# Recurrent gates by blocks of 64 features: two stacked float32r passes in place of one float32 product, issued in steps

## The chip, the core and the metric

The kernel runs on one core of one Trainium2 chip. The metric is the device time of one execution in microseconds (us), from the first to the last instruction with the launch around it. Before the change it is 2330.84 us, the median of three runs (2327.64, 2333.63 and 2330.84).

## The reference

The reference is a backbone of two layers. Each layer normalises and modulates 1280 tokens (256 of context, 1024 latent), multiplies them by one wide input weight, feeds four parallel branches (attention, a diagonal state space model called S5, a gated recurrence called RG-LRU, and pooling), gates and projects each branch, sums them and adds the result to the stream. The change touches the RG-LRU, whose gates are two block-diagonal products with four blocks of 64 features:

```python
def _rglru_states(x, h0, lam, w_a, b_a, w_x, b_x, reverse):
    r = jax.nn.sigmoid(_block_diag(x, w_a, b_a))
    i = jax.nn.sigmoid(_block_diag(x, w_x, b_x))
    log_a = -LRU_C * r * jax.nn.softplus(-lam)
    a = jnp.exp(log_a)
    b = jnp.sqrt(-jnp.expm1(2.0 * log_a)) * (i * x)
    return _real_scan(a, b, h0, reverse)
```

It runs in both directions over the sequence, and the sum of both is the branch. Outputs are float32.

## The kernel before, in words

Features lie on the 128 partitions and tokens along the free axis, in three chunks of 256, 512 and 512 tokens (`CH`; the first is the context). A big product keeps float32 accuracy by splitting each operand into a high part in the format float32r and a low part, the rest; `gemm` (L165) then makes three passes for each 128 rows of the contraction: low weights by high input, high by low, high by high. `hgemm` does this for one tile of 128 output features by one chunk with eight such groups, so 24 passes, into a PSUM bank of pool `pg` (two banks). Weights come by `load_w` (L158): a DMA into a ring of two raw tiles (`wr`), a copy by ScalarE to the high part and a subtraction by VectorE to the low part (`wh` and `wl`, four tiles each).

The order within a layer is written in `layer` (L1124): `mla_in`, `mla_kv`, `s5_in` and `lru_in` (input products and what follows on them), then `lru`, `cq_in` (the query latent), `mla_q` (queries), `pool_in`, `pool` with two `gate` tiles between its halves, then `attention`, the other six gates, the S5 branch, the logits of the first merge branch, `merge` and `out_proj`. A program orders the instructions of each engine ahead of time by priority, which is the order in the text except where `hp` raises it, and lets an engine take later work that its own costs call ready. On the chip each engine then keeps that order and waits where an input is late. The gates, and after them the logits, depend on nothing but the modulated input and a weight tile.

`lru` (L584) first computes constants of the recurrence on small tiles and loads `wg`, all gate weights of the layer, as 128 by 128 matrices that hold two blocks of 64 on the diagonal and zeros elsewhere. For each half of the features (f) and each direction (d), four pairs a layer, it does the following. For each chunk and each of the two gates, one float32 matmul of 128 by 128 weights with `xl` writes a bank (pool `pm`, two banks, for the first gate; pool `pS`, three banks, for the second), and ScalarE's tanh writes it to `l1` (tr) or `l2` (ti). Over all 1280 tokens then come exp, tanh and square on ScalarE, a multiply on VectorE, a square root on ScalarE (with a table load before and after), two multiplies and a scan on VectorE. `l1` to `l4` have one buffer each, so the next pair's tanh waits for the scan before. `pool` uses `l1` to `l3` after that. Scratch memory is a stack of pools: `pr` and `pa` for the part up to the pooling, in whose place `p5` (S5), `pt` (attention), `pc` (merge) and `pd` (output projection) come later, a tile there waiting for the tiles that lay in its bytes before. `stream` and `whl` are never released.

Of the kernel before, what the change touches and what calls it, by code (L numbers as in the profile page):

```python
# [16 lines left out]
F32 = mybir.dt.float32  # L17
F32R = mybir.dt.float32r
# [21 lines left out]


V_BADA, V_G, V_QN, V_KVN, V_QG, V_KG, V_KRG = 0, 24, 32, 34, 35, 37, 38
V_D, V_CW, V_CB, V_LAM, V_BA, V_BX, V_PB, V_PS = 39, 41, 49, 51, 55, 59, 63, 65
NV = 67

def view(ap, *dims):

# [16 lines left out]
class Net:  # L64
# [90 lines left out]
        self.act(hi, src, AF.Identity, scale=gain)  # L155
        self.stt(lo, src, gain, hi.bitcast(F32), ALU.mult, ALU.subtract)

    def load_w(self, src, nk, small=False):  # L158

        m = src.shape[1] // nk  # L160
        out = []
        with self.hp():
            for i in range(0, nk * m, 512):
                n = min(512, nk * m - i)
                raw = self.wraw.tile([128, 512], F32, tag="wr", name=self.name("wr"))  # L165
                th, tl, w, kw = ("wph", "wpl", 256, {"bufs": 2}) if small else ("wh", "wl", 512, {})
                hi = self.whl.tile([128, w], F32R, tag=th, name=self.name(th), **kw)
                lo = self.whl.tile([128, w], F32R, tag=tl, name=self.name(tl), **kw)
                self.dma(raw[:, 0:n], src[:, i:i + n])
                self.split(hi[:, 0:n], lo[:, 0:n], raw[:, 0:n])  # L170
                out += [(hi[:, c:c + m], lo[:, c:c + m]) for c in range(0, n, m)]
        return out
# [254 lines left out]
                self.act(vv[:, 256 * i:256 * i + 256], ps[:, 256 * i:256 * i + 256], AF.Identity, scale=rkv[:, t + i:t + i + 1])  # L427
            self.dma(m["vD"][:, t:t + 2], view(vv, 2, 4, 64))

    def cq_in(self, l, m, lat, pa):  # L430

        vec, sv = self.vec[l], m["sums"]
        m["cq"] = [view(self.t(pa, n_, 2 * NT, dt=F32R), 2, NT) for n_ in ("lat", "lat2")]
        sq0 = self.t(pa, "xp", 1312, 2)
        for f in range(2):
            w = self.load_w(self.I["w_in"][l, 1 + f], NK)
            for ci in lat:
                s0, n = CH[ci]
                ps = self.hgemm(w, ci)
                sq = sq0[:, s0:s0 + n] if f == 0 else self.sc(n)  # L440
                with self.hp():
                    self.gain_split(m["cq"][0][:, f, s0:s0 + n], m["cq"][1][:, f, s0:s0 + n], ps, vec[:, V_QN + f:V_QN + f + 1])
                    self.act(sq, ps, AF.Square)
                if f == 1:
                    with self.hp():
                        self.tt(sq, sq, sq0[:, s0:s0 + n], ALU.add)
                    self.tok_sums(sv[:, 2, s0 // 128:(s0 + n) // 128], [sq], self.ones)

    def mla_q(self, l, m, lat, pa):

# [131 lines left out]
        return out  # L582

    def lru(self, l, xls, oD, outs, pa, pr):  # L584
        nc, I, vec = self.nc, self.I, self.vec[l]
        sp = self.t(pa, "lsp", 36)
        lam = vec[:, V_LAM:V_LAM + 4]
        e, z, z2, acc, p4, m4 = (sp[:, 4 * i:4 * i + 4] for i in range(6))
        hba = sp[:, 24:32]
        self.stt(e, lam, -1.0, lam, ALU.mult, ALU.max)  # L590
        self.act(e, e, AF.Exp, scale=-1.0)
        self.ts(z, e, 2.0, None, ALU.add, None)
        nc.vector.reciprocal(out=z, in_=z)
        self.tt(z, z, e, ALU.mult)
        self.tt(z2, z, z, ALU.mult)
        nc.vector.memset(acc, 1.0 / 17)
        for d in (15, 13, 11, 9, 7, 5, 3, 1):
            self.tt(acc, acc, z2, ALU.mult)
            self.ts(acc, acc, 1.0 / d, None, ALU.add, None)
        self.tt(acc, acc, z, ALU.mult)  # L600
        self.ts(z2, lam, -1.0, 0.0, ALU.mult, ALU.max)
# [3 lines left out]
        self.ts(hba, vec[:, V_BA:V_BA + 8], 0.5, None, ALU.mult, None)  # L605
        wg = self.t(pa, "wg", 1024)
        self.dma(wg, I["w_lru"][l])
        wgv = view(wg, 2, 2, 2, 128)
        for f in range(2):
            xl = xls[f]  # L610
            y = self.t(pr, "ly", NT)
            for d in range(2):
                c = 2 * d + f
                col = lambda a: a[:, c:c + 1]
                tr, ti, a, th = (self.t(pr, n_, w_)[:, 0:NT] for n_, w_ in (("l1", 1312), ("l2", 1312), ("l3", 8 * SC), ("l4", 8 * SC)))
                for s0, n in CH:
                    for g, dst in ((0, tr), (1, ti)):
                        ps = (self.pS() if g else self.ps())[:, 0:n]
                        self.mm(ps, wgv[:, d, g, f], xl[:, s0:s0 + n])
                        self.act(dst[:, s0:s0 + n], ps, AF.Tanh, bias=hba[:, 4 * g + c:4 * g + c + 1], scale=0.5)  # L620
                self.act(a, tr, AF.Exp, bias=col(m4), scale=col(m4))
                self.act(th, tr, AF.Tanh, bias=col(p4), scale=col(p4))
                self.act(tr, a, AF.Square)
                self.stt(th, tr, 1.0, th, ALU.add, ALU.mult)
                self.act(th, th, AF.Sqrt, scale=0.25)
                self.stt(ti, ti, 1.0, xl, ALU.add, ALU.mult)
                self.tt(ti, ti, th, ALU.mult)
                scan = nc.vector.tensor_tensor_scan
                if d == 0:
# [7 lines left out]
            o0 = CH[outs[0]][0]  # L637
            self.dma(oD[f][:, o0:], y[:, o0:])


    def pool_in(self, l, lat, pa):

        out = []
        for f in range(2):
            w = self.load_w(self.I["w_in"][l, 5 + f], NK)
            xp = self.t(pa, "xp", 1312, 2)
            for c, n in ((0, 8), (264, 16), (1304, 8)):
                self.nc.gpsimd.memset(xp[:, c:c + n], 0.0)
            for ci in lat:
                s0, n = CH[ci]  # L650
                ps = self.hgemm(w, ci)
                off = s0 + 8 + (16 if ci else 0)
                with self.hp():
                    self.act(xp[:, off:off + n], ps, AF.Copy)
            out.append(xp)
        return out

# [362 lines left out]
    def merge(self, l, lat, oD, gD, tD, pc, s5):  # L1020
# [5 lines left out]
        for bi, b in enumerate(ORDER):  # L1026
# [3 lines left out]
            for ci in lat:  # L1030
                s0, n = CH[ci]
                for f in range(2):
                    with self.hp(2000):
                        o, gt = (self.stream.tile([128, 512], F32, tag="og", name=self.name("og"), bufs=2)[:, 0:n] for _ in range(2))
                        self.dma(o, oD[b][f][:, s0:s0 + n])
                        self.dma(gt, gD[b][f][:, s0:s0 + n])
                        self.stt(o, o, BSCALE[b], gt, ALU.mult, ALU.mult)
# [1 line left out]
            for j in range(NK):  # L1039
                if bi > 0:  # L1040
                    w = self.load_w(I["w_in"][l, 17 + 8 * b + j], NK)
                else:
                    a0 = CH[lat[0]][0]
                    self.dma(y[j][:, a0:], tD[j][:, a0:])
                wp = self.load_w(I["w_branch"][l, b, j], 2, True)
                for ci in lat if j < NK - 1 else [1] + [c for c in lat if c != 1]:
                    s0, n = CH[ci]
                    if bi > 0:
# [40 lines left out]
    def out_proj(self, l, groups, xsrc, pd, xs, acc, bg):  # L1089
        last = l == DEPTH - 1  # L1090
        for grp in groups:
# [4 lines left out]
            for j in range(NK):  # L1096
                w = self.load_w(self.I["w_out"][l, j], NK)
                for ci in grp:
                    s0, n = CH[ci]
                    c = 1 if ci == 0 else 0  # L1100
                    with self.hp(2000):
                        x0 = self.stream.tile([128, 512], F32, tag="og", name=self.name("ox"), bufs=2)[:, 0:n]
                        self.dma(x0, xsrc[:, j, s0:s0 + n])
                    ps = self.hgemm(w, ci)
                    x = x0 if last else xs[ci][:, j]
# [18 lines left out]
    def layer(self, l, pre):  # L1124
# [4 lines left out]
        with self.phase("pr") as pr, self.phase("pa") as pa:  # L1129
# [2 lines left out]
            self.mla_kv(l, m, pa)  # L1132
            uF, uD = self.s5_in(l, pr)
            xl = self.lru_in(l, pa, pads)
            self.lru(l, xl, oD[LRUB], lat, pa, pr)
            self.cq_in(l, m, lat, pa)
            self.mla_q(l, m, lat, pa)
            xp = self.pool_in(l, lat, pa)
            gates = ((b, f) for b in ORDER for f in range(2))
            for _ in self.pool(l, xp, oD[POOLB], lat, pa, pr):  # L1140
                b, f = next(gates)
# [203 lines left out]
def _blockdiag(w):  # L1345
    out = np.zeros((128, 128), np.float32)
    out[:64, :64] = w[0]
    out[64:, 64:] = w[1]
    return out


def _layout(a):
# [14 lines left out]
    for l in range(DEPTH):  # L1367
# [13 lines left out]
            [_fv(a["b_ada"][l]), _fv(a["norm_g"][l]), _fv(a["mla_q_norm"][l]), _fv(a["mla_kv_norm"][l]),  # L1381
             qg, kgn[:, None], krg[:, None], _fv(a["s5_d"][l]),
             np.concatenate([_fv(a["lru_conv_w"][l][k]) for k in range(4)], 1), _fv(a["lru_conv_b"][l]),
             two(a["lru_lambda"][l]), two(a["lru_b_a"][l]), two(a["lru_b_x"][l]),
             _fv(a["pool_b"][l]), _fv(a["pool_scale"][l])], 1))
        ukv = a["mla_w_ukv"][l].reshape(128, 4, 128)
        out["w_ukv"].append(np.concatenate([ukv[:, :, :64].reshape(128, 256), ukv[:, :, 64:].reshape(128, 256)], 1))
# [2 lines left out]
        uq = np.stack([np.concatenate([no, ro][::1 - 2 * (h % 2)], 2)[:, h] for h in range(4)], 1)  # L1390
        out["w_uq"].append(uq.reshape(2, 128, 2, 256).transpose(2, 1, 0, 3).reshape(2, 128, 512))
        out["w_lru"].append(np.concatenate(
            [_blockdiag(a[n][l, d, 2 * f:2 * f + 2]) for d in range(2) for n in ("lru_w_a", "lru_w_x") for f in range(2)], 1))
# [29 lines left out]
```

## Time and profile before

| | before |
|---|---|
| median of 3 runs | 2330.84 us |
| profiled execution | 2328.08 us |
| its span, first to last instruction | 2326.3 us |
| TensorE busy | 2267.7 us |
| VectorE busy | 1547.8 us |
| ScalarE busy | 969.2 us |
| GpSimd busy | 208.3 us |
| mean granted TensorE clock | 0.994 of full speed |

The profile lists for each engine the time in which it ran an instruction. Matmuls are pipelined: the duration of one includes its way through the array, so the cost of a matmul in a dense stretch is read from the distance of the starts. PE is TensorE, DVE is VectorE, ACT is ScalarE, SPq the queue that issues the DMAs. `pm`, `pS`, `pg` and `pP` are PSUM banks by their pool; `l` stands for `l1` to `l4`.

### The profile page before, as it was taken

What the parts mean: (1) busy time and instruction counts of PE and PEld (TensorE: products, weight loads), DVE (VectorE), ACT (ScalarE), POOL (GpSimd) and SP (SyncE); (2) the same over time, 40 slices, a digit from 0 to 9 for tenths busy, and PEclk for the clock granted to TensorE, in tenths of its full rate; (3) what the DMA queues carried; (4) which work ended last, traced back from release to release, by engine and by line L of the source; (5) the groups of instructions that cost most, each with busy time, mean ns of one, the idle gap of its engine ahead of it and who ended that gap; (6) DMA issues with size and microseconds to landing.
All of it is one profiled execution on the core that took longest, in us unless ns stands there. A gap on an engine that the chain in (4) does not pass through costs nothing. (4 is left out here: it accounts for less than half of the span.)

```text
span 2326.3 us, 33035 instructions
## 1 busy us (share of the span) xinstructions
PE 2267.7 (97%) x11680; PEld 1848.0 (79%) x11680; DVE 1547.8 (67%) x3524; ACT 969.2 (42%) x1966; POOL 208.3 (9%) x261
## 2 busy tenths in 40 slices
PE   8899999999999999999999999999999999999999
PEld 3687878888788888788888787778888788877887
DVE  5664769676877888656455745688667978863243
ACT  4646656665312222312243445756664232322131
POOL 0000000000001111111112100000000011111100
PEclk9999999999999999999999999999999999999999
DMA  8141242211534223433234332242213431332134
GB/s 278 56 157 40 103 123 67 76 56 54 174 94 122 74 77 109 127 94 104 96 100 157 115 116 70 99 132 73 70 56 116 118 105 53 86 110 85 49 115 157
DMA packets 215750, 236.34 MB, mean 102 GB/s; under 512 B 78112, under 2 KB 141344, under 8 KB 215584
## 3 DMA queue, kind: packets, MB, share of 16 engines
q1 hardware_dynamic: 215072, 234.19, 32.4%
q8 instruction: 92, 1.51, 0.3%
q0 software_dynamic: 512, 0.03, 0.1%
q14 instruction: 74, 0.61, 0.1%
HBM read 175.70 MB, written 58.46 MB: 101 GB/s over the span
## 5 line engine op out<-in xcount | busy, mean ns | idle before, releaser
L135 PE MATMUL pg<-h,wh 128*128 128x512 f32 (+1 forms) x4608 | 1346.8, 374 | 0.2 <-DVE h L117 0.2
L135 PEld LDWEIGHTS pg<-h,wh 128*128 128x128 f32 x4608 | 828.7, 188 | 154.6 <-issue 4.5
L135 PE MATMUL pg<-h,wl 128*128 128x512 f32 (+2 forms) x2304 | 871.1, 378 | 1.8 <-DVE wl L117 1.6
L135 PEld LDWEIGHTS pg<-h,wl 128*128 128x128 f32 (+1 forms) x2304 | 434.0, 188 | 81.1 <-issue 3.6
L117 DVE TENSOR_TENSOR wl<-wr,wh 128x512 fp32r<-128x512 f32 x268 | 190.3, 712 | 172.0 <-ACT wh L132 171.1
L132 ACT ACTIVATE wh<-wr 128x512 fp32r<-128x512 f32 x268 | 167.9, 628 | 277.9 <-PE pg L135 150.8
L132 ACT ACTIVATE st<-pg 128x512 f32<-128x512 f32 (+1 forms) x200 | 110.4, 552 | 350.5 <-PE pg L135 343.1
L117 POOL TENSOR_TENSOR y<-y,st 128x512 f32<-128x512 f32 (+1 forms) x120 | 153.1, 1276 | 733.8 <-DVE st L120 696.3
L135 PE MATMUL pm<-b,wph 128*128 128x512 f32 (+1 forms) x640 | 184.4, 372 | 1.6 <-DVE b L117 1.6
L132 ACT ACTIVATE P<-pS,sm,qs 128x512 f32<-128x512 f32 (+1 forms) x200 | 138.6, 702 | 45.3 <-DVE sm L124 43.2
L135 PE MATMUL pS<-k,q 128*128 128x512 f32 (+1 forms) x600 | 145.4, 365 | 0.6 <-DVE q L117 0.4
L120 DVE SCALAR_TENSOR_TENSOR st<-st,pm 128x512 f32<-128x512 f32 (+1 forms) x120 | 75.5, 629 | 105.4 <-PE pm L135 104.9
L135 PEld LDWEIGHTS pm<-b,wph 128*128 128x128 f32 x640 | 115.7, 188 | 24.5 <-DVE b L117 3.1
L135 PE MATMUL pP<-pt,v 128*128 128x256 f32 x656 | 126.9, 301 | 3.4 <-DVE pt L117 1.2
L135 PEld LDWEIGHTS pP<-pt,v 128*128 128x128 f32 x656 | 99.1, 188 | 35.1 <-ACT pt L132 21.5
L117 DVE TENSOR_TENSOR pt<-pm,pt 128x512 fp32r<-128x512 f32 x164 | 107.0, 683 | 26.5 <-ACT pt L132 25.8
L135 PE MATMUL pm<-b,wpl 128*128 128x256 f32 (+1 forms) x320 | 120.1, 376 | 4.5 <-ACT b L132 2.6
L518 DVE TENSOR_REDUCE sm<-pS 128x1 f32<-128x512 f32 (+1 forms) x200 | 113.4, 587 | 14.3 <-PE pS L135 13.0
L132 ACT ACTIVATE pt<-pm 128x512 fp32r<-128x512 f32 x164 | 91.0, 600 | 70.5 <-PE pm L138 70.1
L135 PEld LDWEIGHTS pS<-k,q 128*128 128x128 f32 x600 | 98.7, 189 | 18.6 <-ACT P L132 4.8
L138 PE MATMUL pm<-ident,P 128*128 128x128 f32 x656 | 106.3, 274 | 0.2 <-ACT P L132 0.2
L120 DVE SCALAR_TENSOR_TENSOR pP<-wa,cv,pP 128x256 f32<-128x256 f32 x196 | 95.3, 486 | 13.9 <-DMA wa<-in_w_ada 10.1
(243 smaller groups left out, 2508.0 us busy)
## 6 DMA issues: line engine op xcount, KB each, us to landing
wr<-in_w_in SPq DMA_DIRECT2D x196, 256.0 KB, 2.7
wa<-in_w_ada SPq DMA_DIRECT2D x96, 256.0 KB, 2.9
wr<-in_w_out SPq DMA_DIRECT2D x64, 256.0 KB, 2.8
gD<-st SPq DMA_DIRECT2D x32, 256.0 KB, 2.0
tD<-st SPq DMA_DIRECT2D x32, 256.0 KB, 2.2
og<-oD SPq DMA_DIRECT2D x32, 256.0 KB, 2.7
og<-gD SPq DMA_DIRECT2D x32, 256.0 KB, 3.0
wr<-in_w_branch SPq DMA_DIRECT2D x64, 128.0 KB, 2.1
```

The lines of the kernel that those rows point to most:

```text
L117: (eng or self.nc.vector).tensor_tensor(out=out, in0=a, in1=b, op=op)
L120: self.nc.vector.scalar_tensor_tensor(out=out, in0=a, scalar=s, in1=b, op0=op0, op1=op1)
L132: self.nc.scalar.activation(out=out, in_=a, func=func, scale=scale, **kw)
L135: self.nc.tensor.matmul(out=out, lhsT=lhsT, rhs=rhs, start=start, stop=stop)
L138: self.nc.tensor.transpose(out=out, in_=in_, identity=ident)
L518: nc.vector.tensor_reduce(out=mx3[:, i:i + 1], in_=S, axis=AX.X, op=ALU.max)
```

## The change

Each recurrent block of 64 features gets its own matmul, whose 128 output columns are both gates of that block side by side. The input of a block is stacked on the partitions: high part on the block's own 64, low part on the other 64 (`xb`). One pass of the low weights over the 64 rows with the high part, and one pass of the high weights, repeated on both halves, over all 128 rows give the same three products as `gemm`. The bias of the second gate is stored in the order in which it now comes out, so `vec` grows by four columns. `lru` becomes a generator with eight steps a layer; `cq_in` and `pool_in` advance it after each latent chunk, and `pool_in` moves ahead of `mla_q`. Gate weights are loaded for each pair, through the raw ring. To make room, the tiles `og`/`ox` and the small weights `wph`/`wpl` move from the permanent pools into `pc` and `pd`.

```diff
-        wg = self.t(pa, "wg", 1024)
-        self.dma(wg, I["w_lru"][l])
-        wgv = view(wg, 2, 2, 2, 128)
+        H = (slice(0, 64), slice(64, 128))
         for f in range(2):
             xl = xls[f]
+            xb = view(self.t(pa, "xb", 2 * NT, dt=F32R), 2, NT)
+            for s0, n in CH:
+                for b in range(2):
+                    src, hi = xl[H[b], s0:s0 + n], xb[H[b], b, s0:s0 + n]
+                    self.act(hi, src, AF.Copy)
+                    self.tt(xb[H[1 - b], b, s0:s0 + n], src, hi.bitcast(F32), ALU.subtract)
...
+                raw = self.wraw.tile([128, 512], F32, tag="wr", name=self.name("wr"))[:, 0:256]
+                wh, wl = (view(self.t(pa, n_, 256, 2, F32R), 2, 128) for n_ in ("wgh", "wgl"))
+                with self.hp():
+                    self.dma(raw, I["w_lru"][l][:, 256 * c:256 * c + 256])
+                    self.split(wh, wl, view(raw, 2, 128))
                 for s0, n in CH:
-                    for g, dst in ((0, tr), (1, ti)):
-                        ps = (self.pS() if g else self.ps())[:, 0:n]
-                        self.mm(ps, wgv[:, d, g, f], xl[:, s0:s0 + n])
-                        self.act(dst[:, s0:s0 + n], ps, AF.Tanh, bias=hba[:, 4 * g + c:4 * g + c + 1], scale=0.5)
+                    cols = slice(s0, s0 + n)
+                    for b in range(2):
+                        o = H[b]
+                        ps = (self.pS() if b else self.ps())[:, 0:n]
+                        self.mm(ps, wl[o, b], xb[o, b, cols], True, False)
+                        self.mm(ps, wh[:, b], xb[:, b, cols], False, True)
+                        self.act(tr[o, cols], ps[o], AF.Tanh, bias=hba[o, c:c + 1], scale=0.5)
+                        e = 4 + 2 * c + b
+                        self.act(ti[o, cols], ps[H[1 - b]], AF.Tanh, bias=hba[H[1 - b], e:e + 1], scale=0.5)
+                    if s0 == CH[1][0]:
+                        yield
...
+                yield
...
-                        o, gt = (self.stream.tile([128, 512], F32, tag="og", name=self.name("og"), bufs=2)[:, 0:n] for _ in range(2))
+                        o, gt = (pc.tile([128, 512], F32, tag="og", name=self.name("og"), bufs=2)[:, 0:n] for _ in range(2))
...
-                wp = self.load_w(I["w_branch"][l, b, j], 2, True)
+                wp = self.load_w(I["w_branch"][l, b, j], 2, pc)
...
-                        x0 = self.stream.tile([128, 512], F32, tag="og", name=self.name("ox"), bufs=2)[:, 0:n]
+                        x0 = pd.tile([128, 512], F32, tag="og", name=self.name("ox"), bufs=2)[:, 0:n]
...
-            self.lru(l, xl, oD[LRUB], lat, pa, pr)
-            self.cq_in(l, m, lat, pa)
+            rec = self.lru(l, xl, oD[LRUB], lat, pa, pr)
+            self.cq_in(l, m, lat, pa, rec)
+            xp = self.pool_in(l, lat, pa, rec)
             self.mla_q(l, m, lat, pa)
-            xp = self.pool_in(l, lat, pa)
```

In `cq_in` and `pool_in` the added lines are `if ci > 0: next(bg)` after each chunk's eviction. On the host, `w_lru` is laid out as both gates of one block side by side, on both halves of the partitions.

## Rows read from the trace of the kernel before

**Rows 1.** The page's part 1: busy us, share of the span, instructions.
```profile
PE 2267.7 (97%) x11680; PEld 1848.0 (79%) x11680; DVE 1547.8 (67%) x3524; ACT 969.2 (42%) x1966; POOL 208.3 (9%) x261
```

**Rows 2.** Waits of PE: waiter, releaser, us in total, times, longest.
```profile
PE pS L135 <- DVE er L117: 11.2, 6, 2.6
PE pP L135 <- DMA wa<-in_w_ada: 10.8, 1, 10.8
PE pS L135 <- ACT h L132: 6.0, 1, 6.0
...
PE pg L135 <- DVE wl L117: 1.6, 2, 1.3
...
PE pS L135 <- ACT l L132: 0.9, 1, 0.9
```

**Rows 3.** Stretches: start:end, length, busy PE, PEld, DVE, ACT, POOL, PEclk, DMA, GB/s.
```profile
168.00:257.00 89.00, 86.31 (x417) 67.09 (x416) 50.71 (x54) 60.94 (x83) 0.37 (x6) 1.00 0.18 59
257.00:315.00 58.00, 57.78 (x308) 47.09 (x306) 35.20 (x85) 27.60 (x46) 0.00 (x0) 1.00 0.47 155
1413.00:1510.00 97.00, 96.58 (x426) 73.06 (x425) 62.76 (x71) 71.03 (x94) 0.37 (x6) 1.00 0.22 75
```

**Rows 4.** PE in order of time: start us, us; input products, first pair's gates.
```profile
160.06 0.28 PE L135 MATMUL pg<-h,wl 128*128 128x256 f32 x1
...
162.89 0.40 PE L135 MATMUL pg<-h,wl 128*128 128x512 f32 x1
...
168.49 0.59 PE L135 MATMUL pm<-xl,wg 128*128 128x256 f32 x2
...
172.78 0.59 PE L135 MATMUL pm<-xl,wg 128*128 128x256 f32 x2
```

**Rows 5.** PE by form: records, busy us, mean ns; gates and a 64-row product.
```profile
L135 PE MATMUL pm<-xl,wg 128*128 128x512 f32 x32 | 16.7, 604 | 0.0
...
L135 PE MATMUL pS<-lat,sel 64*128 64x512 f32 x8 | 3.9, 602 | 0.0
```

**Rows 6.** ACT in order of time: tanh evictions of the recurrent gates, layer 0.
```profile
169.70 0.47 ACT L132 ACTIVATE l<-pm,lsp 128x256 f32<-128x256 f32 x1
170.06 0.47 ACT L132 ACTIVATE l<-pS,lsp 128x256 f32<-128x256 f32 x1
...
201.50 0.47 ACT L132 ACTIVATE l<-pm,lsp 128x256 f32<-128x256 f32 x1
...
219.21 0.47 ACT L132 ACTIVATE l<-pS,lsp 128x256 f32<-128x256 f32 x1 [2.83 <-DVE l L634]
...
237.73 0.69 ACT L132 ACTIVATE l<-pm,lsp 128x512 f32<-128x512 f32 x1
238.30 0.70 ACT L132 ACTIVATE l<-pS,lsp 128x512 f32<-128x512 f32 x1
```

**Rows 7.** ACT by form, 168 to 257 us: count, busy us, mean ns.
```profile
L132 ACT ACTIVATE xp<-pg 128x512 f32<-128x512 f32 x6 | 3.5, 589 | 3.3 <-PE pg L135 2.2 <-DVE lat L120 1.1
...
L132 ACT ACTIVATE sc<-pS,vec 64x512 f32<-64x512 f32 x2 | 1.4, 677 | 0.7 <-PE pP L135 0.7
...
L132 ACT ACTIVATE sc<-pS 128x256 f32<-128x256 f32 x2 | 0.7, 369 | 0.0
```

**Rows 8.** DVE by form, 168 to 257 us: count, busy us, mean ns.
```profile
L117 DVE TENSOR_TENSOR wl<-wr,wh 128x512 fp32r<-128x512 f32 x9 | 6.2, 686 | 3.0 <-ACT wh L132 3.0
```

**Rows 9.** SPq in order of time: the recurrence's last store in layer 0.
```profile
257.03 0.32 SPq L111 DMA_DIRECT2D oD<-ly  x1
```

**Rows 10.** PE in order of time: the first product of layer 0's attention.
```profile
315.16 1.21 PE L135 MATMUL pS<-k,q 128*128 128x256 f32 x7 [0.36 <-DVE q L117]
```

**Rows 11.** Stretch just behind the 6.0 us wait (columns as Rows 3).
```profile
81.00:84.00 3.00, 2.75 (x7) 2.23 (x8) 2.36 (x10) 2.86 (x8) 0.00 (x0) 0.50 0.52 173
```

**Rows 12.** DVE at the end of layer 0's merge: a split, first use of ox.
```profile
1181.32 0.68 DVE L117 TENSOR_TENSOR h<-y,h 128x512 fp32r<-128x512 f32 x1
...
1186.20 0.75 DVE L120 SCALAR_TENSOR_TENSOR x<-pg,mod,ox 128x512 f32<-128x512 f32 x1 [0.39 <-PE pg L135]
```

More of the change, by code (lines that the diff above doesn't have):

```diff
@@ L42 @@
 V_BADA, V_G, V_QN, V_KVN, V_QG, V_KG, V_KRG = 0, 24, 32, 34, 35, 37, 38
-V_D, V_CW, V_CB, V_LAM, V_BA, V_BX, V_PB, V_PS = 39, 41, 49, 51, 55, 59, 63, 65
-NV = 67
+V_D, V_CW, V_CB, V_LAM, V_BA, V_BX, V_PB, V_PS = 39, 41, 49, 51, 55, 59, 67, 69
+NV = 71
 def view(ap, *dims):
@@ L156, in gain_split, with load_w @@
         self.stt(lo, src, gain, hi.bitcast(F32), ALU.mult, ALU.subtract)
-    def load_w(self, src, nk, small=False):
+    def load_w(self, src, nk, small=None):
         m = src.shape[1] // nk
@@ L166, in load_w @@
                 th, tl, w, kw = ("wph", "wpl", 256, {"bufs": 2}) if small else ("wh", "wl", 512, {})
-                hi = self.whl.tile([128, w], F32R, tag=th, name=self.name(th), **kw)
-                lo = self.whl.tile([128, w], F32R, tag=tl, name=self.name(tl), **kw)
+                pool = small or self.whl
+                hi = pool.tile([128, w], F32R, tag=th, name=self.name(th), **kw)
+                lo = pool.tile([128, w], F32R, tag=tl, name=self.name(tl), **kw)
                 self.dma(raw[:, 0:n], src[:, i:i + n])
@@ L428, in mla_kv, with cq_in @@
             self.dma(m["vD"][:, t:t + 2], view(vv, 2, 4, 64))
-    def cq_in(self, l, m, lat, pa):
+    def cq_in(self, l, m, lat, pa, bg):
         vec, sv = self.vec[l], m["sums"]
@@ L447, in cq_in @@
                     self.tok_sums(sv[:, 2, s0 // 128:(s0 + n) // 128], [sq], self.ones)
+                if ci > 0:
+                    next(bg)
     def mla_q(self, l, m, lat, pa):
@@ L588, in lru @@
         e, z, z2, acc, p4, m4 = (sp[:, 4 * i:4 * i + 4] for i in range(6))
-        hba = sp[:, 24:32]
+        hba = sp[:, 24:36]
         self.stt(e, lam, -1.0, lam, ALU.mult, ALU.max)
@@ L604, in lru @@
         self.ts(m4, acc, -4.0, None, ALU.mult, None)
-        self.ts(hba, vec[:, V_BA:V_BA + 8], 0.5, None, ALU.mult, None)
-        wg = self.t(pa, "wg", 1024)
-        self.dma(wg, I["w_lru"][l])
-        wgv = view(wg, 2, 2, 2, 128)
+        self.ts(hba, vec[:, V_BA:V_BA + 12], 0.5, None, ALU.mult, None)
+        H = (slice(0, 64), slice(64, 128))
         for f in range(2):
             xl = xls[f]
+            xb = view(self.t(pa, "xb", 2 * NT, dt=F32R), 2, NT)
[4 more added lines that the diff above has]
+                    self.tt(xb[H[1 - b], b, s0:s0 + n], src, hi.bitcast(F32), ALU.subtract)
             y = self.t(pr, "ly", NT)
@@ L636, in lru, with pool_in @@
                     self.tt(y, y, tr, ALU.add)
-            o0 = CH[outs[0]][0]
-            self.dma(oD[f][:, o0:], y[:, o0:])
-    def pool_in(self, l, lat, pa):
+                    o0 = CH[outs[0]][0]
+                    self.dma(oD[f][:, o0:], y[:, o0:])
+                yield
+    def pool_in(self, l, lat, pa, bg):
         out = []
@@ L654, in pool_in @@
                     self.act(xp[:, off:off + n], ps, AF.Copy)
+                if ci > 0:
+                    next(bg)
             out.append(xp)
@@ L1383, in _layout @@
              np.concatenate([_fv(a["lru_conv_w"][l][k]) for k in range(4)], 1), _fv(a["lru_conv_b"][l]),
-             two(a["lru_lambda"][l]), two(a["lru_b_a"][l]), two(a["lru_b_x"][l]),
+             two(a["lru_lambda"][l]), two(a["lru_b_a"][l]), np.tile(a["lru_b_x"][l].reshape(8, 64).T, (2, 1)),
              _fv(a["pool_b"][l]), _fv(a["pool_scale"][l])], 1))
@@ L1392, in _layout @@
         out["w_lru"].append(np.concatenate(
-            [_blockdiag(a[n][l, d, 2 * f:2 * f + 2]) for d in range(2) for n in ("lru_w_a", "lru_w_x") for f in range(2)], 1))
+            [np.tile(np.concatenate([a[n][l, d, 2 * f + b] for n in ("lru_w_a", "lru_w_x")[::1 - 2 * b]], 1), (2, 1))
+             for d in range(2) for f in range(2) for b in range(2)], 1))
         out["w_pool"].append(np.concatenate([_blockdiag(a["pool_w"][l, 2 * f:2 * f + 2]) for f in range(2)], 1))
```

## The prediction

> **What bounds the kernel now.** I read the page's busy times first: TensorE is busy for 2267.7 us, 97% of the span, VectorE for 67%, ScalarE for 42% [rows 1]. TensorE is the bound, and an instruction taken off it is worth its time as long as no wait takes its place. Then the waits of PE: the great ones lie at the start (10.8 and 6.0 us) and in the S5 branch (11.2 us in six), none in the recurrence; there the two longest are 1.3 us for a weight split and 0.9 us for a tanh eviction [rows 2]. Then the stretches of the recurrence, because ScalarE, idle on average, is not idle there: 60.94 of 89 us in layer 0 and 71.03 of 97 us in layer 1, with PE busy for 86.31 and 96.58 us at full clock [rows 3]. So the gate matmuls are paid in full on the engine that sets the end, and ScalarE, which evicts them, is the engine that could take over.
>
> **The gate matmuls.** The first pair starts at 168.49 us and the second at 172.78: 4.29 us for one pair, which is two gates by 2.145 us (0.43 for 256 tokens and 0.86 for each 512) [rows 4]. There are 2 layers x 2 halves x 2 directions = 8 pairs (the 32 records of 512 tokens in `pm` are two for each of 16 matmuls, so the float32 product runs as two halves of 0.43 us [rows 5]): 8 x 4.29 = 34.3 us.
>
> After the change a pair is two blocks by two passes, each over 256, 512 and 512 columns. What a float32r pass costs in a dense chain is in the input products: 24 of 512 columns from 162.89 to 168.49, 5.60 / 24 = 0.233 us, and 24 of 256 columns from 160.06 to 162.89, 0.118 us [rows 4]. Four passes by (0.118 + 2 x 0.233) are 2.34 us a pair, 18.7 us in all. PE loses 34.3 - 18.7 = 15.6 us of work.
>
> One of the two passes has only 64 rows, and no float32r pass with 64 rows is in the trace. The nearest row is the float32 product with 64 rows, with a mean of 602 ns for 512 columns against 604 with 128 rows [rows 5]: rows cost nothing and save nothing, so I take 0.233. From above, were it as slow as a float32 half (0.43 and 0.215), it would add 16 x (2 x 0.196 + 0.097) = 7.8 us; from below it could at most vanish, another 16 x 0.584 = 9.3 us off, which the row gives no ground for. The Trainium skill ("TensorE: Matmul & The Clock Gate", section Back-to-back issue gap) has a warm matmul of N columns take N/2.4 + 2.5 ns, 216 ns for 512; by that, as an estimate, the sum would be 17 us saved in place of 15.6. The trace's 233 decides.
>
> **Evictions and stacking on ScalarE.** Each bank now holds both gates of one block and leaves in two tanhs of 64 partitions. A half-height ACTIVATE is no shorter: 64x512 takes 677 ns, and the full-height tanh 0.69 [rows 6, 7]. Back to back they follow at 0.57 us (512) and 0.36 (256) [rows 6]. Six more a pair: 2 x (0.36 + 2 x 0.57) = 3.0 us. Stacking adds six copies for each half of the features, 2 x (0.37 + 2 x 0.59) = 3.1 us [rows 7], so 1.55 a pair, and the split of a pair's 256 weight columns 0.37. About 4.9 us a pair, 19.7 us a layer. VectorE gets six subtractions a half (0.69 us for 512 columns [rows 8], a little over half of it for 256), 3.6 us, and 0.4 a pair for weights: 8.8 us a layer on an engine with 38 us idle there [rows 3].
>
> So in layer 0 ScalarE would have 61 + 20 = 81 us of work in a stretch that has shrunk from 89 to 81. It can't all stay there, and the recurrence must end later. Before, pairs two and three begin 17.7 us apart (201.50 and 219.21), bound by the chain tanh, exp, root, scan through the single buffers `l1` to `l4` [rows 6]. With 3.0 us more it is near 21. The first step now waits for the stacking and for two chunks of `cq_in` (8.4 us), so it starts near 180 rather than 170; four pairs and a second stacking end near 268, where the last store was issued at 257 [rows 9]. The pooling comes behind it, and attention, whose tiles lie where `xp` and `xl` lay, at some 315 to 325 us (before 315 [rows 10]), although PE has 7.8 us less to do until then. Some 8 to 18 us of gate tiles must fill that. They exist: in layer 0 a gate is 3 chunks, 14 us, six of them stand behind attention in the text, and the program may take them early. In the 58 us behind the recurrence PE was busy for 57.78 and ScalarE only for 27.60 [rows 3], so the late tanhs find room.
>
> **Steps and waits.** Each step issues at most four banks (two of `pm`, two of the three of `pS`), then an input product of 5.6 us, in which ScalarE can do the eight half-height tanhs of 0.36 to 0.57 (some 4 us). A step's first matmul waits for stacked input and for free banks; behind it on PE stand the next products of `cq_in` and `pool_in`, which are ready, so each such wait is lost. Before, four pairs a layer cost 2.2 us of such waits in layer 0 [rows 2]; with twice the steps and a fuller ScalarE I charge 1.8 us a layer, 3.5 us in all, between 0 and 12 (16 steps at 0.75).
>
> **The moved parts.** `pool_in` ahead of `mla_q` changes which of two ready products comes first, with its four weight loads; the query stores on SP and the `mla_q` evictions come later by up to 28 us of `pool_in`, and attention waits for them. I cost this at nothing beyond the delay above, under the same cover of gates. The gate weights go from one DMA of 512 KB to four of 128 KB a layer through the two raw buffers, a place each ahead of a weight load; four tiles of `wh` are two products ahead, 28 us: nothing. `og` and `wph` in `pc` lie behind 60 KB of `y` and `b`, on bytes free since the pooling: nothing. `ox` in layer 0's `pd` comes behind 27 KB of `x` and `acc` and so lies on the first `y`. That one is split for the last time by about 1181 us, and the first use of `ox` was at 1186.20 [rows 12]: a load has 4 us to land before anybody waits, and PE then still has a second bank of `pg` to fill. Nothing, at most 2.5 us.
>
> **Sum.** Off 15.6, on 3.5: 12.1 us. The profiled execution takes 2328.1 us (span 2326.3 and 1.8 around it), so 2316; it lies 2.8 us under the median, so on the runs' scale 2318, -0.5%.
>
> **The rivals.**
> 1. Given back. Attention starts no earlier and has fewer gates beside it; PE then waits in S5, where VectorE already ends its waits (11.2 us [rows 2]). Or the 64-row pass costs the 7.8. Either gives back 8 to 16 us: 2326 to 2331. For it: the chain of the recurrence gets longer, not shorter. Against it: the logits of eight tiles stand behind the gates as more filler.
> 2. Slower, ScalarE as the bound. If the written order puts steps of the recurrence on PE in the tempo of the text and not of ScalarE, PE waits for `l1`, `l2` and banks in front of ready work. ScalarE's 81 us stand against the 65 us of PE's gates, `cq_in` and `pool_in` in layer 0 (9.4 + 4 x 14) and similarly against 54 in layer 1: 16 to 20 us lost a layer, 35 in all, less the 15.6: 2350. It decides when no gate is taken ahead of attention. Long waits cost more than themselves: behind the 6.0 us wait the granted clock was 0.50 for 3 us, the 1.2 GHz level [rows 11], 1.5 us each time. The Trainium skill (same page, section HAM oscillation) says too that idle gaps throttle the array; the trace agrees. Against the rival: ScalarE at 69% made PE wait for 2.2 us only.
> 3. Better: the finer mix also takes away the waits that stood in the stretch, or the 64-row pass is cheaper: 2308 to 2311.
>
> **How the numbers follow.** Forecast 0.64 (2311 to 2324), rival 1 0.19, rival 2 0.12, rival 3 0.05. A measurement tells 0.3%, 7 us, from no change: 2323.8 and below is faster. That is nearly all of the forecast, rival 3 and a little of rival 1: 0.71. Same 0.18, slower 0.11 (rival 2 without its mildest part). Range 2309 to 2332.
>
> **What would show it.** Right: passes on `xb` 0.233 us apart for 512 columns, 64 rows or 128; PE busy down by 15 us; half-height tanhs near 0.69; the last `oD` store 5 to 20 us later; `st` of gates ahead of the first attention product. Wrong: waits of PE on ACT `l` or `xb` over 8 us in sum, a clock under 0.95 between 168 and 260 us, or waits on `er` above 20 us.

## The result and the profile after

After the change the kernel takes 2346.58 us (median of 4 runs) against 2329.52 for the kernel before on the same chip: ratio 1.0075, 95% interval 1.0062 to 1.0087. It is slower by 17 us, where 13 us less was forecast and the range ended at 2332. The profiled execution took 2347.9 us, its span 2346.2.

Part 1 of the page after (columns as in [rows 1]):

```profile
PE 2280.6 (97%) x11680; PEld 1850.6 (79%) x11680; DVE 1567.7 (67%) x3556; ACT 1020.5 (43%) x2048; POOL 208.2 (9%) x261
```

TensorE was to lose 15 us of work; it is busy for 13 us more. ScalarE has 51 us more, some 25 a layer instead of the 20 worked out.

The first step of the recurrence in layer 0, PE in order of time, after (start us, us; it answers to the gates in [rows 4]):

```profile
180.20 0.38 PE L135 MATMUL pm<-xb,wgl 64*128 64x256 f32 x1
180.51 0.38 PE L135 MATMUL pm<-xb,wgh 128*128 128x256 f32 x1
180.83 0.38 PE L135 MATMUL pS<-xb,wgl 64*128 64x256 f32 x1
181.14 0.39 PE L135 MATMUL pS<-xb,wgh 128*128 128x256 f32 x1
181.45 0.50 PE L135 MATMUL pm<-xb,wgl 64*128 64x512 f32 x1
181.88 0.49 PE L135 MATMUL pm<-xb,wgh 128*128 128x512 f32 x1
182.31 0.50 PE L135 MATMUL pS<-xb,wgl 64*128 64x512 f32 x1
182.74 0.51 PE L135 MATMUL pS<-xb,wgh 128*128 128x512 f32 x1
183.08 0.40 PE L135 MATMUL pg<-h,wl 128*128 128x512 f32 x1
```

Read the distances of the starts: 0.43 us for each pass of 512 columns, 0.31 for 256, for the low pass (`wgl`, 64 rows) and for the high pass (`wgh`, 128 rows) alike. A dense pass was 0.233 and 0.118 [rows 4], so each takes some 0.195 more. This step took 2.88 us, the pair's second 1.64 (four passes from 188.76 to 190.40): 4.52 a pair, 8 x 4.52 = 36.2 us, where 34.3 was before and 18.7 was forecast. That is the price where the passes follow each other. Later steps send most of them in twos or singly between input products, whose own passes beside them then take longer as well. With what these neighbours take above their usual distance, all gate passes cost 38 us in this trace; the float32 products before, counted in the same way, cost 35.

The three stretches of [rows 3], after:

```profile
168.00:257.00 89.00, 87.76 (x408) 66.50 (x407) 46.96 (x61) 64.89 (x95) 0.38 (x6) 0.98 0.22 69
257.00:315.00 58.00, 57.45 (x303) 46.61 (x302) 40.28 (x56) 39.37 (x57) 0.00 (x0) 1.00 0.29 104
1413.00:1510.00 97.00, 96.27 (x395) 70.38 (x395) 54.60 (x63) 70.26 (x100) 0.38 (x6) 1.00 0.20 64
```

(PEclk is the granted clock of TensorE: 1.00 is its level of 2.4 GHz, 0.50 that of 1.2 GHz.) PE has hardly a gap here: the loss isn't a long stall in the recurrence. But in the same time it gets through fewer matmuls (408 for 417, 395 for 426), and ScalarE's work has moved behind 257 us (39.37 for 27.60). The recurrence's last store, [rows 9], is at 287.67 (257.03 before; 268 forecast), and the first attention product, [rows 10], comes 23 us later in layer 0 and, in layer 1, 42 us later (1574.08 for 1532.26):

```profile
287.67 0.32 SPq L111 DMA_DIRECT2D oD<-ly  x1
...
337.83 0.98 PE L135 MATMUL pS<-k,q 128*128 128x256 f32 x6
...
1574.08 2.01 PE L135 MATMUL pS<-k,q 128*128 128x512 f32 x9 [0.33 <-DVE q L117]
```

PE did not idle meanwhile: it took gate tiles. The passes on `pg` (the big products; `st` evicts a gate) up to attention, in attention, and from there to the merge of layer 0, first before, then after (start:end, length, busy PE with count, PEclk, DMA share, GB/s):

```profile
0.00:315.16 315.16, 172.44 (x824) 0.99 0.41 131
315.16:561.00 245.84, 118.29 (x510) 1.00 0.21 64
561.00:673.90 112.90, 91.12 (x443) 1.00 0.47 140
```

```profile
0.00:337.75 337.75, 190.68 (x911) 0.98 0.39 125
337.75:583.10 245.35, 117.53 (x504) 1.00 0.21 64
583.10:682.80 99.70, 75.90 (x362) 1.00 0.50 149
```

So 87 passes more stand ahead of attention and 81 fewer behind it, in the S5 branch. The waits of PE, after, that answer to [rows 2]:

```profile
PE pP L135 <- DMA wa<-in_w_ada: 11.2, 1, 11.2
PE pS L135 <- DVE er L117: 8.7, 5, 3.3
PE pm L135 <- ACT b L132: 6.4, 5, 2.9
PE pS L135 <- DVE wl L117: 6.0, 1, 6.0
...
PE pS L135 <- ACT wk L132: 3.3, 3, 1.5
PE pm L135 <- DVE b L117: 3.1, 3, 2.1
...
PE pS L135 <- ACT l L132: 0.6, 2, 0.3
```

Waits for the recurrence itself (`l`) are under 1 us. What grew is at the S5 branch's end and the merge's start: ACT `b` from 2.6 to 6.4, DVE `b` from 1.6 to 3.1, ACT `wk` from 0.6 to 3.3, while DVE `er` fell from 11.2 to 8.7. The same three before:

```profile
PE pm L135 <- ACT b L132: 2.6, 4, 0.7
PE pm L135 <- DVE b L117: 1.6, 3, 0.8
...
PE pS L135 <- ACT wk L132: 0.6, 1, 0.6
```

All that stands behind attention, in layer 0 up to the last product of the merge's branches and in layer 1 up to the end, before and then after:

```profile
561.00:1178.50 617.50, 604.31 (x3182) 510.03 (x3181) 443.74 (x949) 167.66 (x358) 91.17 (x81) 0.99 0.35 106
1764.30:2326.30 562.00, 548.86 (x2465) 443.99 (x2464) 343.39 (x639) 157.67 (x317) 72.18 (x57) 0.99 0.34 102
```

```profile
583.10:1190.60 607.50, 590.62 (x3103) 497.59 (x3102) 444.75 (x946) 165.57 (x353) 90.07 (x80) 0.99 0.35 106
1801.80:2346.10 544.30, 528.41 (x2366) 426.52 (x2364) 341.42 (x636) 153.79 (x309) 73.11 (x57) 0.99 0.34 103
```

PE is idle here for 32.8 us instead of 26.3, though it has fewer matmuls to do. A long wait can cost more than its length. The stretch around a wait of 2.9 us for ACT `b`, which ended at 1897.52:

```profile
1896.00:1904.00 8.00, 6.48 (x19) 5.33 (x20) 6.82 (x13) 1.05 (x2) 1.40 (x1) 0.57 0.40 131
```

The granted clock is 0.57 here, so most of the stretch ran at the lower level. The Trainium skill ("TensorE: Matmul & The Clock Gate", section HAM oscillation) says that gaps throttle the array; the trace agrees, 0.57 behind the 2.9 us gap. Over the whole execution the mean granted clock is 0.991 instead of 0.994, some 7 us of work not done (an estimate: 0.009 x 2346 - 0.006 x 2326).

So of the 19.9 us between the two spans some 17 can be placed: 7.0 us more of idle PE in all (65.6 for 58.6), some 7 us by the lower clock, and 3 us by the gate passes, which were to save 15.6.

### The profile page after: what moved, and what is told of

Its sections match the earlier page's. It is cut to its first block, busy times and chain, and to the rows that moved or that the text cites. A ratio compares the mean times of both kernels' runs of the same rounds, so it can differ in the third digit from the quotient of the medians.

```text
span 2346.2 us, 33185 instructions
## 1 busy us (share of the span) xinstructions
PE 2280.6 (97%) x11680; PEld 1850.6 (79%) x11680; DVE 1567.7 (67%) x3556; ACT 1020.5 (43%) x2048; POOL 208.2 (9%) x261
## 5 line engine op out<-in xcount | busy, mean ns | idle before, releaser
L135 PEld LDWEIGHTS pP<-pt,v 128*128 128x128 f32 x656 | 99.2, 188 | 36.2 <-ACT pt L132 23.6
L117 DVE TENSOR_TENSOR pt<-pm,pt 128x512 fp32r<-128x512 f32 x164 | 107.1, 682 | 21.2 <-ACT pt L132 19.9
```

Source lines behind the costliest of these rows:

```text
L117: (eng or self.nc.vector).tensor_tensor(out=out, in0=a, in1=b, op=op)
L135: self.nc.tensor.matmul(out=out, lhsT=lhsT, rhs=rhs, start=start, stop=stop)
```

## The experiments

Each was timed beside runs of the kernel before; a ratio is to these. The letters of the theories are those of each quoted text and can differ between texts.

### The price of a change of row height

**All rows in the low pass** (against the kernel after). The other 64 rows then bring a negligible further term, low by low:

```diff
-                        self.mm(ps, wl[o, b], xb[o, b, cols], True, False)
+                        self.mm(ps, wl[:, b], xb[:, b, cols], True, False)
```

> The changed kernel with one edit: the low-weight pass runs over all 128 rows (low weights by high and low input, so the tiny low-by-low product is added). Theory A, a pass costs 0.195 us more when its row count differs from that of the pass before it: the 96 passes on xb fall from 0.43 to 0.233 us (512 columns) and from 0.31 to 0.118 (256), their sum from 33.5 to about 18.7 us, and the time by about 15 us, 2346.6 to about 2332. Rival, the passes are slow because the stacked input or the evictions are late: spacing stays at 0.43 and the time within 5 us of 2346.

2335.89 us, ratio 1.0024 (1.0013 to 1.0034): 10.7 us less than after, by one operand. PE in order of time, this run:

```profile
180.75 0.39 PE L135 MATMUL pm<-xb,wgl 128*128 128x512 f32 x1
180.98 0.39 PE L135 MATMUL pm<-xb,wgh 128*128 128x512 f32 x1
181.21 0.40 PE L135 MATMUL pS<-xb,wgl 128*128 128x512 f32 x1
181.44 0.39 PE L135 MATMUL pS<-xb,wgh 128*128 128x512 f32 x1
```

The passes stand 0.23 us apart; a pair takes 2.32 us, 18.6 in all, which is the forecast's 18.7. So the price hangs on 64 rows next to 128, not on float32r, the stacking or the banks. With their neighbours the passes cost 24 us in this trace, where they cost 38 after. But these 14 us of TensorE gave 10.7, less than theory A's 15, and this version is still 5 us slower than before, with 11 us less of gate passes: there is a second cause. Its passes on `pg` stand as in the kernel after (911 ahead of attention in layer 0, 362 behind it).

**The low passes of a chunk together**, then the high ones (against after):

```diff
-                    for b in range(2):
-                        o = H[b]
-                        ps = (self.pS() if b else self.ps())[:, 0:n]
-                        self.mm(ps, wl[o, b], xb[o, b, cols], True, False)
-                        self.mm(ps, wh[:, b], xb[:, b, cols], False, True)
+                    pss = [(self.pS() if b else self.ps())[:, 0:n] for b in range(2)]
+                    for b in range(2):
+                        self.mm(pss[b], wl[H[b], b], xb[H[b], b, cols], True, False)
+                    for b in range(2):
+                        self.mm(pss[b], wh[:, b], xb[:, b, cols], False, True)
...
```

> The kernel after, with the two low (64-row) passes of a chunk first and then the two high (128-row) passes, so that the height changes twice a chunk instead of four times. If each change of height costs: some 96 of 192 changes go, 96 x (2 x 0.195 + 0.19)/3 or so, about 15 us of extra falls to 8, gate passes from 33.5 to about 26 us, time 2337 to 2341. If each pass that has or follows 64 rows costs by itself (the second low pass too), gate passes stay near 31 to 33.5 us, time 2344 to 2348.

2343.35 us, ratio 1.0065 (1.0042 to 1.0088). PE in order of time:

```profile
180.64 0.49 PE L135 MATMUL pm<-xb,wgl 64*128 64x512 f32 x1
180.64 0.49 PE L135 MATMUL pS<-xb,wgl 64*128 64x512 f32 x1
181.06 0.50 PE L135 MATMUL pm<-xb,wgh 128*128 128x512 f32 x1
181.41 0.40 PE L135 MATMUL pS<-xb,wgh 128*128 128x512 f32 x1
181.64 0.39 PE L135 MATMUL pg<-h,wl 128*128 128x512 f32 x1
```

The two low passes, on different halves of the rows, start at the same time; the change to 128 rows and back costs once for the group (0.42 and 0.35 instead of 0.233), and the second high pass is at 0.23 again. A group of four takes 1.00 us instead of 1.64. So the change costs, not the pass. But only ten such groups, 40 of the 96 passes, stand together in the trace; the others come in twos and singly, as after. All passes with their neighbours cost some 33.5 us instead of 38, and the time falls by about 3 us, to a value between the two theories' ranges: this run shows the mechanism in the starts, not in the time.

### Order and scratch

**Steps alone**: before, with `lru` as a generator, `next(bg)` in `cq_in` and `pool_in`, and `pool_in` ahead of `mla_q`.

> The kernel before with the steps and the order of the change alone; float32 gates, scratch tiles where they were. Theory B: slower than before by 10 to 17 us (2340 to 2347), with the waits of PE on b in the last merge (2.9 us near 1897) and the half clock behind them. Theory C: within 4 us of before (2326 to 2334).

2329.44 us, ratio 0.9991 (0.9978 to 1.0005): no change that can be told.

**Scratch alone**: before, with `og`, `ox`, `wph` and `wpl` in `pc` and `pd`.

> The kernel before with og/ox and the small weights moved to pc and pd alone. Theory C, og now comes late in merge: slower by 5 to 17 us, with PE waits on ACT b of 6 us in sum against 2.6. Theory B: within 4 us of before.

2332.31 us, ratio 1.0000 (0.9989 to 1.0011). Neither part moves the time by itself, beside float32 gates, as the prediction had it.

**The new gates without steps**, after with `for _ in self.lru(...): pass` in the old place and `mla_q` ahead of `pool_in`:

> The changed kernel with the recurrence issued in one go at its old place, the queries ahead of pool_in again; stacked gates and moved scratch tiles stay. Theory B, the steps and the order bring the new waits and the clock losses behind them (about 15 of the 17 us): time near 2332. Theory C, the moved scratch tiles or the gates themselves bring them: time stays near 2346.

2366.45 us, ratio 1.0150 (1.0134 to 1.0167). Both theories missed. The steps and the order are worth some 20 us to these gates; they are not what makes them slow.

### ScalarE

**Half-height tanhs alone** (against before; TensorE's products, the order in the text and memory stay):

```diff
-                        self.act(dst[:, s0:s0 + n], ps, AF.Tanh, bias=hba[:, 4 * g + c:4 * g + c + 1], scale=0.5)
+                        for o in (slice(0, 64), slice(64, 128)):
+                            self.act(dst[o, s0:s0 + n], ps[o], AF.Tanh, bias=hba[o, 4 * g + c:4 * g + c + 1], scale=0.5)
```

> The kernel before with one edit: each tanh of a gate bank is two tanhs of 64 partitions; TensorE's work, the order and the memory are those of before. ScalarE gets 3.0 us more a pair, 12 us a layer. Theory C (the time follows the end of the recurrence's chain on ScalarE and VectorE, because attention, S5 and the merge stand behind it and the product tiles that can fill TensorE meanwhile are a fixed number): first attention product 8 to 15 us later in each layer, fewer products on pg between attention and the merge, 2334 to 2345 us. Rival D (the loss hangs on the new passes, their stacking or their order): 2329 to 2332 us, as before.

2343.49 us, ratio 1.0048 (1.0032 to 1.0064): 11 us for 31 us more on ScalarE. First attention product, layers 0 and 1:

```profile
322.61 0.98 PE L135 MATMUL pS<-k,q 128*128 128x256 f32 x6
...
1551.67 1.53 PE L135 MATMUL pS<-k,q 128*128 128x512 f32 x6
```

7 and 19 us later than before. This is the second cause. In this run it doesn't work by the place of the filler: 836 passes on `pg` stand ahead of attention in layer 0 for 824, and 436 behind it for 443. PE stops for the tanhs in the recurrence itself, for example here:

```profile
176.73 1.12 PE L135 MATMUL pS<-xl,wg 128*128 128x512 f32 x2 [0.27 <-ACT l L132]
178.13 1.12 PE L135 MATMUL pm<-xl,wg 128*128 128x512 f32 x2 [0.28 <-ACT l L132]
```

Waits for `l` come to 3.5 us (0.9 before), and the float32 products, now spread between input products, cost 40 us with their neighbours instead of 35.

**A float32 product in place of the two passes** (against after; the stacked input stays, unused):

```diff
-                        self.mm(ps, wl[o, b], xb[o, b, cols], True, False)
-                        self.mm(ps, wh[:, b], xb[:, b, cols], False, True)
+                        self.mm(ps, wf[o, b], xl[o, cols])
...
```

> The kernel after, with each pair of float32r passes replaced by one float32 product of the block's 64 rows with xl (wf[o, b] by xl[o, cols]); stacking stays, its output unused; half-height tanhs, steps and moved scratch stay. TensorE's gate work is then that of before, 8 x 4.29 = 34.3 us, and no 64-row pass stands next to a 128-row pass but at the ends of a block. Theory A (the rest of the loss is ScalarE's longer work in the recurrence, which draws gate tiles forward and leaves S5 and the merge without filler): 2342 to 2348 us, with waits of pm on ACT b of 5 us or more. Rival B (the rest comes with the float32r passes themselves): 2329 to 2333 us.

2361.83 us, ratio 1.0139 (1.0113 to 1.0164). The rival (2329 to 2333 us) falls: without float32r passes the loss is there. Theory A's size missed too, and the premise: the float32 products of the two blocks ran beside each other (176.56 and 176.57 us), so that two chunks took 1.49 us (176.56 to 178.05) where they took 2.57 before; and later ones, between 128-row passes, take 1.05 us to the next start instead of 0.86, so this run still pays for changes of height. In one stretch the clock stayed at its lower level:

```profile
1457.00:1474.00 17.00, 16.73 (x41) 10.87 (x42) 7.37 (x10) 10.99 (x17) 0.18 (x3) 0.50 0.14 39
```

After had 1.00 and 75 matmuls there. PE is busy nearly throughout, behind a 2.8 us wait, and loses some 8 us (half of 17, an estimate); why the clock stayed low for so long is open.

**Three passes at full height** (against after): weights as 128 by 128 block diagonals again, so a bank leaves in one tanh.

```diff
...
+                        self.mm(ps, wl[:, g], xb[:, 0, cols], True, False)
+                        self.mm(ps, wh[:, g], xb[:, 1, cols], False, False)
+                        self.mm(ps, wh[:, g], xb[:, 0, cols], False, True)
+                        self.act(dst[:, cols], ps, AF.Tanh, bias=hba[:, 4 * g + c:4 * g + c + 1], scale=0.5)
...
```

> The kernel after, with the 128 by 128 block-diagonal weights of before, split in high and low, and three float32r passes over all 128 rows (low by high, high by low, high by high); xl is split at full height, and each bank leaves in one full-height tanh as before. Steps and moved scratch stay. TensorE: 6 passes x (0.118 + 2 x 0.233) = 3.5 us a pair, 28.0 in all, 6.3 less than before. ScalarE: 3 copies a half and 0.37 a pair for weights, about 4.6 us a layer more than before instead of 19.7. Theory A (ScalarE's load is what is given back): 2322 to 2327 us, passes on xb 0.233 us apart. Rival B (the passes bring the loss): 2335 to 2340 us.

2330.43 us, ratio 1.0004 (0.9992 to 1.0016). Passes stand 0.23 us apart (3.5 us a pair); ScalarE is busy 6 us more than before. The loss is gone, but so is the gain: both theories missed, by 3 and by 5 us.

**The copies on GpSimd or VectorE** instead of ScalarE, first for the version with all rows in the low pass, then for the three passes:

```diff
-                    self.act(hi, src, AF.Copy)
+                    nc.gpsimd.tensor_copy(out=hi, in_=src)
...
```

> The kernel with the low pass over all 128 rows, with the stacking copies and the copies of the gate weights on GpSimd instead of ScalarE: ScalarE has 7.7 us a layer less. GpSimd's copy was never timed at this size; its 128x512 addition takes 1.40 us, so the six copies of a half may take up to 7 us. Theory A: 2329 to 2333 us (a third to a half of the loss of 2335.9 goes). Rival B: 2335 to 2337 us.

2338.97 us, ratio 1.0034 (1.0019 to 1.0049), above both ranges. On VectorE:

> The kernel after with the low pass over all 128 rows, and the stacking copies and copies of the gate weights on VectorE instead of ScalarE (on GpSimd they took 0.80 us each and nothing was won). ScalarE keeps only the half-height tanhs, 24 us more than before as in the run with these alone, which cost 11 us; TensorE 15.6 us less. Theory C: 2324 to 2331 us. Rival E: 2338 to 2343 us, as with the half-height tanhs alone.

2337.25 us, ratio 1.0026 (1.0018 to 1.0035), just below rival E's range. The copies bring nothing that can be measured: with them on ScalarE it was 1.0024. Against the half-height tanhs alone (1.0048), dense float32r passes, 15.6 us less by the forecast's sum, gave 3 to 6 us in these three runs.

> The kernel with full-height gates in three float32r passes and steps, with the high copies of the input and of the gate weights on VectorE instead of ScalarE, so that ScalarE has no more work than before. TensorE 6.3 us less than before. Theory C (ScalarE's load in this stretch is what is given back): 2323 to 2327 us. Rival E (what TensorE is spared in this stretch is not worth its time at all, since the tiles that fill it run out later): 2329 to 2332 us.

2328.74 us, ratio 0.9994 (0.9983 to 1.0004): no measurable gain from 6.3 us less of TensorE.

### How the added work reaches the end

**Shorter chain**: two buffers for `l1` and `l2`, with float32 gates, with and without steps.

> The kernel before with steps, moved scratch (neither of which moved the time by itself) and two buffers each for l1 and l2, so that the next pair's tanhs need not wait for the scan before; the gates stay float32, TensorE's work is that of before. Theory C: the recurrence gets shorter by 3 to 8 us a layer and the time falls to 2320 to 2327 us although TensorE has nothing less to do. Rival (the end of the recurrence has slack, attention waits for something else): 2329 to 2332 us.

> The kernel before with moved scratch and two buffers each for l1 and l2, in the order of before (no steps). Theory C: recurrence from 170 us to some 225 to 232 us instead of 237, 2320 to 2328 us. Rival (slack at the end of the recurrence): 2329 to 2332 us.

2333.30 us, ratio 1.0008 (0.9996 to 1.0020), and 2341.86 us, ratio 1.0037 (1.0021 to 1.0053). In the second, the recurrence's last store comes 6 us earlier than before (250.84 for 257.03), and attention 4 us later (319.59 for 315.16). Both runs are slower than theory C has it, and the first is 1 us above its rival's range. So theory C, in which the chain's end alone sets the time, falls. (The second buffers also shift the scratch memory behind them, which no run separates.)

**Three passes at once**, `for _ in rec: pass` ahead of `cq_in`:

> The kernel with full-height gates in three float32r passes, but the recurrence issued in one go ahead of the query latent (no steps); pooling input still ahead of the queries. TensorE has 6.3 us less than before; the recurrence starts near 170 instead of 178.6 us. Theory C: recurrence and first attention product some 8 us earlier, 2318 to 2327 us. Rival (one go puts TensorE behind ScalarE's chain, as it did with the gates of the kernel after, where it cost 20 us): 2335 to 2350 us.

2342.69 us, ratio 1.0050 (1.0032 to 1.0067). The same against C: against the three passes in steps an earlier start (171.9 us for 178.6) and a later attention (319.9 for 313.5).

**Only the place of gate tiles** (against before):

```diff
                 b, f = next(gates)
                 self.gate(l, b, f, lat, gD[b])
+            for _ in range(2):
+                b, f = next(gates)
+                self.gate(l, b, f, lat, gD[b])
```

> The kernel before with one edit in the order: two more gate tiles (four instead of two) stand ahead of attention in the text. All work is that of before; in the order that the program makes of it, 912 product passes of layer 0 stand ahead of the first attention product instead of 824 (the kernel after has 911) and 54 more in layer 1 (after: 114 more). Theory F (product tiles that are used up ahead of attention are missing as filler between attention and the merge, and that is the way in which the kernel after loses its time beside the height changes): first attention product some 20 us later, longer waits in the S5 branch and at the merge's start, 2336 to 2342 us. Rival G (the shift of tiles is a symptom; the longer ScalarE work itself costs): 2329 to 2332 us.

2338.52 us, ratio 1.0030 (1.0019 to 1.0042): 7 to 8 us, with all work as before. Passes on `pg` as above, this run, and then its S5 stretch (before had 81.82 us, 443 matmuls and 1.00 in the same 84 us, with attention over 17 us earlier):

```profile
0.00:332.20 332.20, 189.85 (x912) 0.99 0.41 131
332.20:578.30 246.10, 117.21 (x502) 1.00 0.20 60
578.30:681.10 102.80, 79.02 (x364) 0.97 0.48 141
```

```profile
586.00:670.00 84.00, 77.91 (x420) 65.94 (x419) 72.02 (x182) 27.25 (x64) 2.42 (x3) 0.96 0.53 158
```

It is the picture of the kernel after, 912 and 364 against 911 and 362, with none of its gates. PE is idle for 62 us in all instead of 59, 3 of them more behind attention in layer 0, and by the mean clocks (0.992 for 0.994) some 5 us go to the lower level.

> The kernel before with one gate tile instead of two ahead of attention in the text: 793 passes of layer 0 ahead of the first attention product instead of 824, 10 less in layer 1. Theory F: attention 5 to 7 us earlier in layer 0, more filler behind it, 2326 to 2330 us. Rival G: 2329 to 2332 us, or slower where the pooling now has too little beside it.

2329.71 us, ratio 0.9990 (0.9979 to 1.0001): attention 7.5 us earlier (307.65), the time inside what can be told from no change and inside both theories' ranges: it decides nothing.

> What the runs point to as a version ahead of both: full-height gates in three float32r passes, their copies on VectorE, steps, and one gate tile instead of two ahead of attention in the text. ScalarE as before, TensorE 6.3 us less, attention not later than before. If both small gains (2.1 and 1.2 us by the medians, neither measurable alone) add: 2326 to 2328 us. If they were scatter: 2329 to 2333 us.

2328.77 us, ratio 0.9988 (0.9976 to 1.0000): the best of all by its ratio, 2.6 us under the kernel before, at the edge of what can be measured and between its two expected ranges.

## Why the prediction was wrong

**The step that failed first** is "rows cost nothing and save nothing, so I take 0.233". It compared mean durations, 602 and 604 ns, which hold the way through the array, where the price is the distance of the starts; and it asked only what such a pass costs among its like, not what it does to its neighbour. The 128-row pass behind it is as slow, which even the upper bound (7.8 us, on the low passes alone) left out. Measured: 36.2 us instead of 18.7 by the first pair, and 38 in the trace as a whole; taking the change of height away gave back 10.7 us of time. The trace of the kernel before had a sign of it, in the very product that the prediction took:

```profile
104.15 1.98 PE L135 MATMUL pS<-lat,sel 64*128 64x512 f32 x4
106.06 0.38 PE L135 MATMUL pS<-lat,wl 128*128 128x256 f32 x1
106.29 0.40 PE L135 MATMUL pS<-lat,wh 128*128 128x256 f32 x2
```

The four records of 64 rows, which stand between products of 32 and of 128 rows, take 1.91 us to the next start instead of 4 x 0.43 = 1.72, and the 128-row pass behind them 0.23 instead of 0.118. The Trainium skill ("TensorEngine Tiling (Array Packing)", section Key Properties) has a rule that fits: a change of the tiling mode drains TensorE, while different tiles can run in parallel. The trace agrees with both halves, some 0.195 us a change and two low passes starting at 180.64; that 64 rows next to 128 are such a change of mode is inferred here. The prediction overlooked it.

**The second failing step** is the cover: "some 8 to 18 us of gate tiles must fill that. They exist", at no price. They do, and PE stayed busy. But the tiles taken were the filler of the S5 branch: 87 passes, 18 us (190.68 - 172.44), in layer 0 and 114 in layer 1. Behind attention PE is then idle for 6.4 us more, and the lower clock costs some 7 us. Rival 1 named the mechanism ("fewer gates beside it; PE then waits in S5") but priced it as a part of the gain. Moving tiles alone cost 7 to 8 us, the half-height tanhs alone 11.

**The sum** by the ratios, each from a pair of runs: half-height tanhs +11; from these to dense float32r passes in steps -6; change of height +12; together the 17 measured. The three lead from one version to the next, so they add up by construction, and the parts were not timed in every combination. What moved the tiles is open in part. With full-height tanhs in steps (three passes, copies on VectorE) the counts of layer 0 are those of before, 824 and 443; with half-height tanhs and two passes over all rows they are 898 and 371. That speaks for the tanhs, but the two differ by 9 us of gate passes as well, and the tanhs alone moved 12 passes. How far the 11 us of the tanhs and the 8 us of moved tiles are the same time isn't shown. Nor is why spared TensorE time counts so unevenly (6.3 us gave at most 2, 15.6 gave 3 to 6, the 14 of the change of height 10.7): that PE only reaches S5 with nothing left to do would fit the small ones, but is only argued.

**Right**: steps and moved scratch cost nothing; the dense price of 0.233 at one height; full-height and half-height tanhs alike at 0.68; waits for `l` and `xb` small (1.4 us in all). **Off in size**: the last store (268 forecast, 287.67), attention (315 to 325 forecast, 337.83). Rival 2, 2350 us, came nearest in time, but by another way, so by luck: PE did not wait for ScalarE in the recurrence. And none of the three signs that were to show the prediction wrong appeared (waits for `l` and `xb` 1.4 us, clock 0.98, `er` 8.7 us): it watched for a stall, and the loss was no stall there.

## What to carry to other kernels

Where matmuls of different row height alternate, price the change between them, in both neighbours; a negligible term that keeps the height was cheaper here. When an engine that is 97% busy is kept so by filler, ask which later stretch that filler was meant for: the busy times show no gap where it is used up, only where it is missing. An added eviction in a stretch full for ScalarE is not free, even where TensorE stays busy meanwhile.

## What the runs showed of the hardware that was not expected

- 64-row and 128-row passes in turn: 0.43 us for 512 columns and 0.31 for 256, against 0.233 and 0.118 at one height; the pass of 128 rows pays as much as that of 64.
- Two 64-row products on different halves of the rows run beside each other, in float32r (both at 180.64) and float32 (176.56 and 176.57).
- A granted clock of 0.50 for 17 us of busy TensorE behind a 2.8 us wait.
